# Gating the output projection's r tiles earlier, beside the last head's output loop

## The chip, the cores and the metric

The kernel runs on one core of one Trainium2 chip. A core has five engines that run side by side, each through its own list of instructions in order: TensorE (PE, matrix multiplication; PEld are its weight loads), VectorE (DVE), ScalarE (ACT), GpSimd (POOL) and SyncE (SP), which here issues nearly all transfers. The metric is device time in microseconds (us), the median of several executions. The profile comes from one more execution with the hardware profiler on.

## The reference

One layer of a sequence model, for 1024 tokens of width 1024, in float32. What the change touches:

```python
h = rmsnorm(x)
q, k, v, r, lr_f, lr_b, u, g_a, g_b = split(h @ w_in)
o = gla(q, k, v, lr_f) + gla reversed (q, k, v, lr_b)   # 4 heads, 256 channels each
o = o * rsqrt(mean(o * o) + eps) * gla_norm             # per head
o = o * silu(r)                                         # the gate
y_a = o @ w_branch_gla
```

Afterwards `y_a` is merged with a pooling branch `y_b` under sigmoid gates, projected and added to `x`, and a SwiGLU block with its own norm follows. The gate `o * silu(r)` is elementwise, so it can be computed in pieces of any order, as soon as a piece of `r` and the same piece of `o` exist.

## The kernel before, in words

**Numbers in two parts.** Every float32 operand of a large matrix product is split in two parts, high (`hh`, `wh`, `trh`) and low (`hl`, `wl`, `trl`). A product is three matmuls: high by high, low by high, high by low (`products`, L271). The high part is a cast on ScalarE, the low part a subtraction on VectorE or GpSimd (`split_to`, L200). `hT` holds the normed input, features on partitions, in 16 tiles: four groups of features, two token halves, high and low.

**The r tiles.** The 1024 columns of `r` are eight tiles of 128. Tiles 0 to 5 are "plain": for each of two token halves of 512, `feature_major` (L297) adds 8 x 3 matmuls into one PSUM bank. Tiles 6 and 7 are computed together as the first "gate unit" (`gunits[0]`), by a Strassen-like scheme: seven products instead of eight, in the order 1, 2, 6, 5, 3, 7, 4, each of 12 matmuls. Products 1, 6, 7 and 4 add onto one bank, 5 and 3 onto another; where a partial sum is wanted, ScalarE first copies it to a `ga` tile (L1497). Products 4 to 7 need differences of blocks of `hT`; these were stored to memory (`f_out`) and come back through `feature_parts` as `hs` tiles, which are split into `trh` and `trl` (L708, L699).

**Beside the plain tiles** runs the attention of the last head (`attention(3)`): decays, a backward pass of states, the scores of each token half (`scores`: a predicated copy L939 on VectorE, then the cast and subtraction that give `p`), and the output loop over eight blocks of 128 tokens (L1013). There each block is an `op` product from `p` and states, with VectorE making a new state `st` and ScalarE scaling it to `sf` and `so`. Its results are scaled, turned, stored to `o_out` and later loaded as `ol` tiles, two per head (`load_o`, L1052).

**The gate** (`gated`, L1205): ScalarE computes Silu of r, VectorE multiplies by the head's `ol` and writes an `o` tile (L1215). Head n gates tiles 2n and 2n+1; once a head's four pieces (two tiles, two token halves) are there, its two `o` tiles are queued for storing to `ob_out`. The first tiles of r come before the head outputs are at hand, so they are copied raw to an `r` tile (L1259) and wait in `raw_r`; each later plain half gates one waiting half (`put_by`, L1223) and then its own, straight from PSUM.

**What sets the order.** The order is written out by hand. All instructions are issued in the order of the Python program, and each engine keeps that order. `pump` (L162) is called after each group of three matmuls. It advances generators, which interleave the attention (`side`), the feature parts (`aside`) and weight splits (`pending`) with the matmuls; `soon` puts steps off by some pumps, `later` and `flush` queue stores on SP. The feature parts begin where the last attention has ended, in plain tile 3 or at tile 4 at the latest.

**Room.** Most tiles (`slot`, L98) share a pool of 39 equal slots: `hT` (16), the last head's q, k, decayed and turned keys, values and states, `r`, `ol`, `o`, `hs`, `trh`, `trl`, `ga`, `fraw` (raw gate weights), `wsum`. A new tile takes a slot that has come free. If that slot's last reader or transfer isn't done, the instruction that first writes the new tile waits for it, and with it everything behind on that engine.

Of the kernel before, what the change touches and what calls it, by code (L numbers as in the profile page):

```python
# [14 lines left out]
AF = mybir.ActivationFunctionType  # L15
# [5 lines left out]
KT = D // P  # L21
# [8 lines left out]
SQ = 32  # L30
# [24 lines left out]
def kernel(  # L55
# [20 lines left out]
    nc = tc.nc  # L76
# [17 lines left out]
    def name(s):  # L94
        count[0] += 1
        return f"{s}_{count[0]}"

    def slot(dtype=F32, shape=(2, HALF), s="slot"):  # L98
        return slots.tile([P, *shape], dtype, tag="slot", name=name(s))

    def t2(width=HALF, dtype=F32, s="t"):
        return tmp.tile([P, width], dtype, tag="t2", name=name(s), padded_shape=[P, HALF + 2 * PAD])
# [45 lines left out]
    side, aside = [], []  # L148
# [6 lines left out]
    def soon(delay, *steps):  # L155
        put_off.extend([delay, step] for step in steps)
# [36 lines left out]
    def finish_side():  # L193
        while side:
            for _ in side[0][0]:
                pass
            side.pop(0)
# [53 lines left out]
    def prepare():  # L251
        if not loaded:
            fetch()
        if loaded:
            ready.append(Weights(loaded.pop(0)))

            credit[0] = -2.0

    def take(ahead=True):

        if not ready:
            prepare()
        w = ready.pop(0)
        w.finish()
        if ahead:
            prepare()
        return w
# [29 lines left out]
    def feature_major(w, act, half, kts=KT):  # L297
        ps = bank(next(mm_banks))
        for k in range(kts):
            mm3(ps[:, :], w(k), act(k, half), k == 0, k == kts - 1)  # L300
        return ps
# [257 lines left out]
    def later(dst, src):  # L559
        deferred.append((dst, src))  # L560

    def flush(eng=nc.sync):
        while deferred:
            eng.dma_start(*deferred.pop(0))
# [101 lines left out]
    def feature_parts():  # L666
        todo = [(p, c) for p in (6, 5, 7, 4) for c in range(2)]
        wholes = []

        def load_sum():  # L670
            if len(wholes) < len(todo):
                p, c = todo[len(wholes)]
                wholes.append(slot(s="hs"))
                nc.sync.dma_start(wholes[-1][:, :, :], f_out[p][:, c])

        yield load_sum, None, None
        for n, (p, c) in enumerate(todo):
            yield load_sum, wholes[n][:, :, :], p
# [47 lines left out]
    def prepare_beside(jobs, every, put=PUT, lag=1, quick=0):  # L726
        aside.append([beside(chain(*jobs), every, put, lag, quick), 1 if quick else every])

    def finish_beside():
        while aside:  # L730
            for _ in aside[0][0]:
                pass
            aside.pop(0)
# [318 lines left out]
    def load_o(h):  # L1052

        o_heads[h] = [slot(s="ol") for _ in range(2)]
        for half in range(2):
            nc.sync.dma_start(o_heads[h][half][:, :, :], o_out[h][half].rearrange("(j p) t -> p j t", p=P))
# [89 lines left out]
    def bank_of(z, p):  # L1146

        if p == 1:
            z.u = bank(ps_mm)
        elif p == 5:  # L1150
            z.x = bank(ps_g)
        return bank(ps_g) if p == 2 else z.u if p in UP else z.x
# [30 lines left out]
    def product(unit, p, ps, right):  # L1183
        for k in range(4):
            mm3(
                ps[:, :], unit(p, k), tuple(t[:, k % 2, :] for t in right[p][k // 2]),
                k == 0 and p in FIRST, k == 3, p not in FIRST,
            )
# [13 lines left out]

    raw_r, oT = [], {}

    def gated(j, half, src):  # L1205

        sr = t2(s="sr")
        nc.scalar.activation(sr[:, :], src, AF.Silu)
        if j // 2 not in oT:
            oT[j // 2] = [slot(s="o") for _ in range(2)], []  # L1210
        tiles, there = oT[j // 2]

        turned = o_heads[j // 2][half][:, j % 2, :].rearrange("p (i n b) -> p n i b", i=4, b=SQ)
        dst, silu = (t.rearrange("p (n i b) -> p n i b", n=4, b=SQ) for t in (tiles[half][:, j % 2, :], sr[:, :]))
        nc.vector.tensor_tensor(dst, turned, silu, op=ALU.mult)  # L1215
        there.append((j, half))
        if len(there) == 4:
            c = j // 2 % 2
            for half, t in enumerate(tiles):
                later(ob_out[j // 4, half][:, 2 * c : 2 * c + 2, :], t[:, :, :])  # L1220
            soon(2, flush)

    def put_by():  # L1223

        if raw_r:
            gated(*raw_r.pop(0))

    BY = 3
    sums_begun = False
    for j in range(KT - 2):  # L1230
        if 2 <= j <= 4:
            load_o(j - 2)
        w = take()
        if j == 4:
            for _ in range(2):
                gunits[0].load()
        if j == 5:
            gates_ahead.step()
        if j < BY:
            whole_r = slot(s="r")  # L1240
        for half in range(2):
            if j >= BY and not sums_begun and (j > BY or not side):
                finish_side()
                finish_beside()
                prepare_beside([feature_parts()], 5, quick=2)
                sums_begun = True
            ps = feature_major(w, hT, half)
            if half == 0:
                flush()
                if j == 4:  # L1250
                    deferred.extend(last_o)
                    flush()
                elif j == 5:
                    load_o(HEADS - 1)
            elif j == KT - 3:
                for _ in range(2):
                    gunits[1].load()
            if j < BY:
                nc.scalar.copy(whole_r[:, half, :], ps[:, :])  # L1259
                raw_r.append((j, half, whole_r[:, half, :]))  # L1260
            else:
                put_by()
                gated(j, half, ps[:, :])
            if j == KT - 3 and half == 0:
                gates_ahead.step()
    for p, i, half in ((1, 0, 0), (2, 1, 0), (3, 1, 1)):
        right[p] = [hT.pair(2 * i + c, half) for c in range(2)]
# [201 lines left out]
    late = []  # L1469

    def finish_late():
        while late:
            late.pop(0)()

    class Gates:
# [12 lines left out]
        def run(self, p):  # L1488
            while len(right.get(p, ())) < 2:
                next(aside[0][0])  # L1490
            ps = bank_of(self, p)
            product(self.unit, p, ps, right)
            ps = ps[:, :]
            finish_late()
            part = {1: (0, 0), 6: (0, 1), 5: (1, 1)}.get(p)
            if part:
                nc.scalar.copy(self.row(part[0])[:, part[1], :], ps)  # L1497
                return
            i, half = {2: (0, 0), 3: (0, 1), 4: (1, 0), 7: (1, 1)}[p]
            done = self.row(i)[:, half, :]  # L1500
            if p != 4:
                add(done, ps, done)
                ps = done
            if self.kind == "r":
                if p == 4:
                    nc.scalar.copy(done, ps)
                late.append(partial(gated, KT - 2 + i, half, done))
                return
            if self.kind != "u":
                nc.scalar.activation(done, ps, AF.Sigmoid)  # L1510
            elif p == 4:
                nc.scalar.copy(done, ps)
            self.done.append((i, half))
            if self.kind == "b" and p in (7, 4):
                for at in self.done:
                    self.pooling(*at)
                self.done = []
# [450 lines left out]
    done = {}  # L1968
# [118 lines left out]
    for at, p in enumerate(OUT_ORDER):  # L2087
# [9 lines left out]
        for i in range(CLOSE if closing else n_of):  # L2097
            n = at * n_of + i
# [57 lines left out]
```

## Time and profile before

| | us |
|---|---|
| median of 3 runs (lowest, highest) | 1383.68 (1383.6, 1384.03) |
| the profiled execution's own time | 1384.49 |
| its span, first to last instruction | 1382.7 |
| TensorE busy | 1358.9 (98%) |
| VectorE / ScalarE / GpSimd busy | 857.4 / 647.3 / 754.5 |
| plain r tile 0 begins; tile 5 ends (TensorE) | 263.7; 348.6 |
| mean granted TensorE clock | 0.995 |

Lines of the profile are read so: the start in us, the duration, the engine, the line of the code, the operation, output<-inputs, shapes and number; in brackets the idle time of the engine before it and what ended it. A line of code can be a helper's, as L202 is for all subtractions. In groups, "us, times, longest" follow the pair that waits and is waited for.

### The profile page before, as it was taken

The page shows a single profiled execution, that of the slowest core. Times are in us where ns is not written, and L with a number is a line of the kernel's source. Part 1 is how long each engine was busy: PE and PEld are TensorE (multiplying, and loading weights), DVE is VectorE, ACT ScalarE, POOL GpSimd, SP SyncE. Part 2 cuts the span into 40 slices and gives each one's busy share as a digit, 9 for nine tenths or more (in the row PEclk, how much of TensorE's full clock was granted, in tenths as well). Part 3 has the DMA queues.
Part 4 walks back from the last instruction along what each step waited for, and adds up shares of the span by engine and source line. Part 5 has one row for each costly group of instructions (what it writes and reads, how often), then busy time and mean ns, then how long its engine had stood idle before and what let it go on. Part 6 is the DMA issues. An engine that isn't in the chain of part 4 may idle for free. (4 is left out here: it accounts for less than half of the span.)

```text
span 1382.7 us, 17799 instructions
## 1 busy us (share of the span) xinstructions
PE 1358.9 (98%) x6246; PEld 1128.5 (82%) x6246; DVE 857.4 (62%) x1054; ACT 647.3 (47%) x1177; POOL 754.5 (55%) x561
## 2 busy tenths in 40 slices
PE   9999999999699999999999999999999999999998
PEld 7888888888488888888888888888888888888886
DVE  6966566655645786687884856555655556343375
ACT  7365666754434445554346633333333334444353
POOL 3323723222488556668665276666666667455454
PEclk9999999999899999999999999999999999999999
DMA  6321623315777668996516355555444447985552
GB/s 225 116 86 54 186 76 104 91 51 183 228 229 253 202 212 282 365 384 219 200 62 233 121 180 175 175 175 175 154 140 142 142 146 259 387 304 188 171 213 77
DMA packets 177563, 254.60 MB, mean 184 GB/s; under 512 B 11672, under 2 KB 103360, under 8 KB 177472
## 3 DMA queue, kind: packets, MB, share of 16 engines
q1 hardware_dynamic: 177328, 253.20, 54.7%
q8 instruction: 49, 0.80, 0.2%
q14 instruction: 42, 0.34, 0.1%
q10 hardware_dynamic: 144, 0.26, 0.0%
HBM read 170.32 MB, written 83.10 MB: 183 GB/s over the span
## 5 line engine op out<-in xcount | busy, mean ns | idle before, releaser
L202 POOL TENSOR_TENSOR wl<-fs,wh 128x512 fp32r<-128x512 f32 x124 | 171.9, 1391 | 165.2 <-ACT wh L201 109.0
L274 PE MATMUL ps<-gh,wh 128*128 128x512 f32 x616 | 240.5, 390 | 0.0
L274 PE MATMUL ps<-gl,wh 128*128 128x512 f32 x616 | 239.8, 389 | 0.3 <-DVE gl L1714 0.3
L274 PE MATMUL ps<-gh,wl 128*128 128x512 f32 x616 | 239.7, 389 | 0.0
L202 POOL TENSOR_TENSOR wl<-fraw,wh 128x512 fp32r<-128x512 f32 x93 | 134.1, 1442 | 80.9 <-ACT wh L201 75.5
L202 POOL TENSOR_TENSOR ol<-gor,oh 128x1024 fp32r<-128x1024 f32 (+1 forms) x42 | 101.6, 2424 | 85.7 <-ACT oh L201 60.0
L274 PE MATMUL ps<-hh,wh 128*128 128x512 f32 x356 | 144.5, 406 | 1.4 <-ACT ga L1497 0.7
L274 PE MATMUL ps<-hh,wl 128*128 128x512 f32 x356 | 139.1, 391 | 1.2 <-POOL wl L202 1.2
L274 PE MATMUL ps<-hl,wh 128*128 128x512 f32 x356 | 138.8, 390 | 0.0
L274 PEld LDWEIGHTS ps<-gl,wh 128*128 128x128 f32 x616 | 115.7, 188 | 24.3 <-DVE gl L1714 0.7
L274 PEld LDWEIGHTS ps<-gh,wl 128*128 128x128 f32 x616 | 115.6, 188 | 24.2
L274 PEld LDWEIGHTS ps<-gh,wh 128*128 128x128 f32 x616 | 115.7, 188 | 24.0 <-DVE sums L1880 0.2
L274 PE MATMUL ps<-oh,oh 128*128 128x512 f32 x308 | 119.8, 389 | 0.0
L274 PE MATMUL ps<-ol,oh 128*128 128x512 f32 x308 | 119.8, 389 | 0.0
L274 PE MATMUL ps<-oh,ol 128*128 128x512 f32 x308 | 119.8, 389 | 0.0
L202 POOL TENSOR_TENSOR wl<-wraw,wh 128x512 fp32r<-128x512 f32 x56 | 92.3, 1677 | 44.8 <-ACT wh L201 44.7
L202 DVE TENSOR_TENSOR ol<-wor,oh 128x1024 fp32r<-128x1024 f32 (+1 forms) x42 | 62.6, 1501 | 67.6 <-ACT oh L201 55.1
L202 POOL TENSOR_TENSOR wl<-raw,wh 128x512 fp32r<-128x512 f32 x34 | 48.1, 1425 | 86.3 <-ACT wh L201 63.4
L201 ACT CAST wh<-fs 128x512 fp32r<-128x512 f32 x124 | 76.0, 614 | 26.4 <-DVE fs L1116 25.4
L274 PEld LDWEIGHTS ps<-hh,wl 128*128 128x128 f32 x356 | 66.8, 188 | 16.2 <-POOL wl L202 2.0
L274 PE MATMUL ps<-trh,wh 128*128 128x512 f32 x176 | 69.6, 396 | 9.9 <-ACT ga L1497 9.9
L274 PEld LDWEIGHTS ps<-hh,wh 128*128 128x128 f32 x356 | 67.0, 188 | 14.4 <-ACT ga L1497 1.2
(278 smaller groups left out, 3085.0 us busy)
## 6 DMA issues: line engine op xcount, KB each, us to landing
fraw<-in_w_ffn_in_dram SPq DMA_DIRECT2D x44, 512.0 KB, 7.2
gor<-g_out SPq DMA_DIRECT2D x35, 512.0 KB, 5.5
fraw<-in_w_in_dram SPq DMA_DIRECT2D x22, 512.0 KB, 5.9
g_out<-s SPq DMA_DIRECT2D x44, 256.0 KB, 2.4
wor<-t_out SPq DMA_DIRECT2D x20, 512.0 KB, 4.0
raw<-in_w_in_dram SPq DMA_DIRECT2D x36, 256.0 KB, 4.4
g_out<-g SPq DMA_DIRECT2D x33, 256.0 KB, 2.5
x<-in_x_dram SPq DMA_DIRECT2D x16, 512.0 KB, 5.4
```

Source lines behind the costliest of these rows:

```text
L201: nc.scalar.copy(hi, src)
L202: eng.tensor_tensor(lo, src, as_f32(hi), op=ALU.subtract)
L274: nc.tensor.matmul(ps, a[i], b[j], start=first and n == 0, stop=last and n == 2, skip_group_check=onto)
```

## The change

The raw wait now ends after two tiles instead of three (`BY`), so plain tile 2 is gated itself and with it tile 0; tile 3 takes tile 1 along; tiles 4 and 5 have no raw tile left to take. The point from which the feature parts may begin stays at tile 3 (`PARTS_FROM`). The loads of the head outputs 0 and 1 move from tiles 2 and 3 to tiles 1 and 2; those of heads 2 and 3 stay at tiles 4 and 5. Of a raw tile, Silu is computed in place, and so it is for the two tiles of the gate unit. In plain tile 5 the second token half comes first.

```diff
-    def gated(j, half, src):
-
-        sr = t2(s="sr")
-        nc.scalar.activation(sr[:, :], src, AF.Silu)
+    def gated(j, half, src, sr=None):
+
+        sr = t2(s="sr")[:, :] if sr is None else sr
+        nc.scalar.activation(sr, src, AF.Silu)
...
-    BY = 3
+    BY, PARTS_FROM = 2, 3
     sums_begun = False
     for j in range(KT - 2):
-        if 2 <= j <= 4:
-            load_o(j - 2)
+        for h in {1: (0,), 2: (1,), 4: (2,)}.get(j, ()):
+            load_o(h)
         w = take()
+        if j < BY:
+            whole_r = slot(s="r")
...
-        if j < BY:
-            whole_r = slot(s="r")
-        for half in range(2):
-            if j >= BY and not sums_begun and (j > BY or not side):
+        for n, half in enumerate(reversed(range(2)) if j == KT - 3 else range(2)):
+            if j >= PARTS_FROM and not sums_begun and (j > PARTS_FROM or not side):
...
             ps = feature_major(w, hT, half)
-            if half == 0:
+            if n == 0:
                 flush()
...
             if j < BY:
                 nc.scalar.copy(whole_r[:, half, :], ps[:, :])
-                raw_r.append((j, half, whole_r[:, half, :]))
+                raw_r.append((j, half, *[whole_r[:, half, :]] * 2))
             else:
                 put_by()
                 gated(j, half, ps[:, :])
-            if j == KT - 3 and half == 0:
+            if j == KT - 3 and n == 0:
                 gates_ahead.step()
...
-                late.append(partial(gated, KT - 2 + i, half, done))
+                late.append(partial(gated, KT - 2 + i, half, done, done))
```

More of the change, by code (lines that the diff above doesn't have):

```diff
@@ L1213, in gated @@
         turned = o_heads[j // 2][half][:, j % 2, :].rearrange("p (i n b) -> p n i b", i=4, b=SQ)
-        dst, silu = (t.rearrange("p (n i b) -> p n i b", n=4, b=SQ) for t in (tiles[half][:, j % 2, :], sr[:, :]))
+        dst, silu = (t.rearrange("p (n i b) -> p n i b", n=4, b=SQ) for t in (tiles[half][:, j % 2, :], sr))
         nc.vector.tensor_tensor(dst, turned, silu, op=ALU.mult)
```

## The prediction

> **What bounds the kernel now.** I read the page first, then the waits of TensorE, then the stretch around its one large wait in windows, and there ScalarE, VectorE and the SP queue in order of time.
>
> ```profile
> span 1382.7 us, 17799 instructions
> PE 1358.9 (98%) x6246; PEld 1128.5 (82%) x6246; DVE 857.4 (62%) x1054; ACT 647.3 (47%) x1177; POOL 754.5 (55%) x561
> PE   9999999999699999999999999999999999999998
> PEclk9999999999899999999999999999999999999999
> ...
> PE ps L274 <- ACT ga L1497: 10.7, 2, 9.9
> PE ps L274 <- POOL wl L202: 2.3, 4, 0.9
> ```
>
> TensorE sets the time: it is busy for 98% of the span. So a change pays only where TensorE waits, and costs only where it makes TensorE wait. Nearly all waiting stands in the eleventh slice, where the r tiles end and the gate products begin: two waits for the copy of a gate sum (`ga`, L1497), one of them 9.9 us.
>
> The windows have, after the stretch in us, the busy time (and the number) of PE, PEld, DVE, ACT and POOL, then PEclk, DMA share and GB/s:
>
> ```profile
> 295.00:303.00 8.00, 8.00 (x51) 7.06 (x49) 3.49 (x7) 2.72 (x7) 1.23 (x1) 1.00 0.00 1
> 337.70:348.60 10.90, 10.90 (x49) 8.70 (x47) 3.38 (x4) 2.90 (x4) 0.00 (x0) 1.00 0.61 183
> 348.60:356.80 8.20, 6.34 (x25) 4.27 (x24) 7.59 (x8) 3.20 (x6) 3.19 (x2) 1.00 0.88 272
> 356.80:366.70 9.90, 0.00 (x0) 0.00 (x0) 7.01 (x7) 5.38 (x9) 4.34 (x3) 0.75 0.78 228
> 366.70:374.90 8.20, 8.19 (x24) 6.28 (x24) 4.99 (x5) 2.74 (x5) 4.96 (x4) 0.67 1.01 350
> ...
> 349.28 0.50 PE L274 MATMUL ps<-hh,wh 128*128 128x512 f32 x1 [0.67 <-ACT wh L201]
> 366.71 0.80 PE L274 MATMUL ps<-trh,wh 128*128 128x512 f32 x1 [9.94 <-ACT ga L1497]
> 375.66 0.50 PE L274 MATMUL ps<-hh,wh 128*128 128x512 f32 x1 [0.73 <-ACT ga L1497]
> ```
>
> The last r tile is 48 matmuls (two token halves of 24) in 10.9 us. The next 48, products 1, 2, 6 and 5 of the first gate unit, lie between 348.6 and 374.9 and take 26.3 us. **15.4 us are lost there**: 9.94 in the wait, some 1.8 in smaller waits before it, 2.8 at the fallen clock after it (8.20 us for 24 matmuls instead of 5.45), the rest in slower starts after each wait. The 0.73 behind that is another matter: product 3 adds onto product 5's bank right after it and must wait for its copy.
>
> Why is the copy at 366.07 so late, when product 1 was done by 353.4? ScalarE and VectorE work in program order:
>
> ```profile
> 345.70 2.01 ACT L708 CAST trh<-hs 128x1024 fp32r<-128x1024 f32 x2 [9.57 <-PE ps L274]
> 348.14 0.58 ACT L1208 ACTIVATE sr<-ps 128x512 f32<-128x512 f32 x1
> 348.62 0.61 ACT L201 CAST wh<-fraw 128x512 fp32r<-128x512 f32 x1
> 357.38 1.04 ACT L708 CAST trh<-hs 128x1024 fp32r<-128x1024 f32 x1 [5.11 <-DMA ob_out<-o]
> 366.07 0.59 ACT L1497 COPY ga<-ps 128x512 f32<-128x512 f32 x1 [1.13 <-DVE fs L1116]
> ...
> 344.40 0.69 DVE L1215 TENSOR_TENSOR o<-ol,sr 128x512 f32<-128x512 f32 x1 [8.03 <-PE ps L274]
> ...
> ob_out<-o SPq DMA_DIRECT2D x8, 512.0 KB, 9.0
> ```
>
> These are waits for room, not for data. A cast to `trh` and a multiplication into an `o` tile wait for matmuls that don't feed them: those matmuls are the last readers of the `h` tiles whose slots they take over. A later cast waits 5.11 us for the store of gated tiles `ob_out`, which had 9.0 us to land. All of it comes from the pool of 39 slots being full. ScalarE stood still for 9.57 and 5.11 us, so the casts of the gate weights (348.62) came when TensorE already wanted them, and product 1's copy stood behind all of it.
>
> **The change part by part.** *Slots.* Before, r tiles 0 to 2 wait raw and are gated one per plain tile from tile 3 on, so pair (2,3) is finished only with tile 5. At the end of tile 3 the old order holds 3 raw tiles, 4 head outputs `ol` and 4 `o` tiles. The new one has gated tiles 0 to 3 by then: 4 `o` tiles are on their way out and nothing else is held, 7 slots fewer, 11 once they have landed. The eight pairs `trh`/`trl`, cast from tile 3 to tile 5, then find slots. Their four stores can go when tile 3's second multiplication ends, 332.9 by the slow pair at 329.37 below, plus the price found below: about 335 instead of 348, so the 9.0 us of landing end near 344, ahead of the critical stretch. Until then they hold up the `hs` loads and the last head's stores behind them on SP, which a full pool held up about as long before. The other edit, second half first in tile 5, frees four `h` slots one half, 24 x 0.227 = 5.45 us, sooner: those of the 8.03 and 9.57 us waits. If ScalarE is no longer blocked for long, the gate's weights are cast during tile 5 and product 1's copy follows its last matmul, 2.7 us (12 matmuls of product 2) before product 6 wants it; the casts then just ahead of it are three of 0.6 us. So I take the **whole 15.4 us** as gone; the lower bound is nothing. The 0.73 stays, its order being unchanged.
>
> *The price in the loop.* Tile 2 is now gated beside the last head's output loop. Two raw copies of 0.57 become four Silus of about 0.6 and four multiplications of 0.69, and the table load moves from 322.7 to the first of them. That is in front of the score chain, which feeds the loop's first `op` product:
>
> ```profile
> 297.89 0.51 ACT L922 ACTIVATE sb<-st,fac 128x256 f32<-128x256 f32 x1 [0.55 <-DVE st L918]
> 298.31 0.57 ACT L1259 COPY r<-ps 128x512 f32<-128x512 f32 x1
> 299.40 0.69 DVE L202 TENSOR_TENSOR p<-sc,p 128x512 fp32r<-128x512 f32 x1 [0.94 <-ACT p L201]
> 301.69 0.28 PE L274 MATMUL op<-vh,p 128*128 128x256 f32 x1
> ...
> 307.97 0.70 DVE L939 COPY_PREDICATED sc<-keep,sc 128x512 f32<-128x512 uint8 x1 [1.81 <-PE sc L934]
> 308.70 0.59 ACT L201 CAST p<-sc 128x512 fp32r<-128x512 f32 x1 [1.01 <-DVE sc L939]
> 309.32 0.69 DVE L202 TENSOR_TENSOR p<-sc,p 128x512 fp32r<-128x512 f32 x1 [0.65 <-ACT p L201]
> 309.92 0.47 DVE L918 SCALAR_TENSOR_TENSOR st<-kv,fac,so 128x256 f32<-128x256 f32 x1
> 310.43 0.51 ACT L922 ACTIVATE sf<-st,fac 128x256 f32<-128x256 f32 x1 [1.15 <-DVE st L918]
> 311.86 0.59 PE L1026 MATMUL op<-sf,qe 128*128 128x256 f32 x2
> ...
> 322.70 1.28 ACT L1208 ACT_TABLE_LOAD   x1
> 324.53 0.58 ACT L1208 ACTIVATE sr<-ps 128x512 f32<-128x512 f32 x1
> 327.07 1.25 DVE L1215 TENSOR_TENSOR o<-ol,sr 128x512 f32<-128x512 f32 x2
> 329.37 3.48 DVE L1215 TENSOR_TENSOR o<-ol,sr 128x512 f32<-128x512 f32 x2
> ```
>
> The r copy stands ahead of the score chain in program order, so both multiplications now stand ahead of COPY_PREDICATED on VectorE. The load can start at 298.40; the second Silu ends 2.41 later, as from 322.70 to 325.11, at 300.8. Its multiplication lets the copy in at about 301.5. The cast follows 0.73 later and the subtraction 0.62 after that, as from 307.97; it ends at 303.55. The `op` matmul that reads it was at 301.69 and had 1.6 us to spare; it now comes at about 303.65. TensorE, and everything queued behind that matmul, waits **2.0 us**. The bounds: 0.7 without the load; 4.2 if the two multiplications take the 3.48 of the slow pair instead of 1.25, though POOL, which was busy beside that pair, is nearly idle here.
>
> At tile 2's second half the same additions, without a load, make the next `st` about 1.0 later against the shifted loop. Its `sf`, ready at 310.94, has 0.92 us until TensorE reads it at 311.86: 0.1 us of wait. With 0.1 for the slower matmuls after a wait the price is **2.2 us**. Tile 3 costs what it cost, less a load that no engine was waiting behind.
>
> The Trainium skill ("ScalarE: Activation LUTs", What ACT_TABLE_LOAD costs) adds a drain of about 1.38 us to the 1.28 us of a load. The trace disagrees: the Silu began 1.30 us after the load's start. By the page the wait would be an estimated 3.4 us, and the time 1.4 higher.
>
> *What is hidden.* One load serves Silu together with the loop's Square and copies: there is none between the Silu's at 769.3 and the Squares at the end.
>
> ```profile
> L166 ACT ACT_TABLE_LOAD  x1: 1283/1283/1283, 769.3 to 769.3; - x1
> L2051 ACT ACTIVATE sq<-x x3: 632/632/632, 1366.5 to 1373.7; 128x512 f32<-128x512 f32 x3
> ...
> 274.06 14.55 SPq L1056 DMA_DIRECT2D ol<-o_out  x2
> ```
>
> The two loads of `ol` move up one r tile each on the SP queue, past the next tile's weights, which they delay by the 1 us of their issue. SP issued tile 3's at 274.06, when TensorE was still ahead of tile 2's 301.69, so that is covered. Before, the second pair held SP for 14.55 us until a slot came free; taken earlier, it should find one. By my count the new order fills the pool exactly (39 of 39) as the loop's first step ends. The four `o` tiles take slots that the loop has already given up, so I cost this at nothing; without that cover VectorE would stop in front of the score chain. Silu in place saves a temporary and no time; in the gate unit too.
>
> The sum: 1384.49 - 15.4 + 2.2 = 1371.3 for the profiled execution (its span is 1.8 less). That one is 0.8 above the median of 1383.68, so against the median I expect **1370.5**.
>
> **The rivals.** *Only the store's wait goes (B).* The casts, differences and copies that ScalarE did from 357.38 to 366.07 may be a chain of their own, with only the 5.11 us saved. Then 4.8 us of the gap stay, the clock still falls (2.8), and 15.4 shrinks to 15.4 - 7.6 = 7.8: 1383.68 - 7.8 + 2.2 = 1378.1. For it: ScalarE's last wait ahead of the copy is for VectorE (1.13). Against: that chain is backlog, since ScalarE had idled 9.57 us just before.
>
> *The loop's wait trips the clock (D).* At its upper bound, 4.2 + 0.2 us, TensorE might restart at half speed as it did after 366.7 and lose those 2.8 us too: 1383.68 - 15.4 + 7.2 = 1375.5. Waits under 1 us left the clock at 1.00. The Trainium skill ("TensorE: Matmul & The Clock Gate", What's actually happening) puts the half rate behind an idle window of about 3.4 us, between my value and my upper bound.
>
> *It doesn't do what it says (C).* If the slots were not the cause and product 1's copy stays where it is, only the price is left: 1383.68 + 2.2 = 1385.9, within what a measurement can tell from no change (0.2%, 2.8 us).
>
> *Slower: the 16 DMA engines become the bound (E).* Place: 335 to 352. Four stores of 0.5 MB now go out together, ahead of the last head's 1 MB, and the `hs` and `fraw` loads queue behind them. The price: 2 MB at the 350 GB/s of the busiest window are 6.0 us by which loads come later; on top of an unremoved gap and the 2.2 that is 1391.9. For it: shares of 0.88, 0.78 and 1.01 around the gap. Against: 0.61 from 337.7 to 348.6. It decides only if the share reaches 1.0 from 335 on and TensorE then waits for casts of loaded tiles, the gap having been a matter of transfers.
>
> **How the numbers follow.** Chances: forecast 0.60, B 0.18, D 0.05, C 0.08, E 0.09. The range: 1367.8 is the forecast with the loop's price at its lower bound (1.5 less) and a further 1.2 for the 0.73 wait and its slow matmuls; upward it takes in D and B, and 2.8 us for a clock that falls once more: 1380.9. C and E lie outside. Faster by over 0.2%: forecast, B and D, 0.83; within 0.2%: C, 0.08; slower: E, 0.09.
>
> **What would show it.** Right: TensorE's largest wait is no longer for `ga` at product 6; the clock stays at 1.00 through tile 5 and the gates; no `trh` cast waits for `ob_out`; a new wait of about 2 us stands at the first `op<-vh,p`, for `p`; the Silu load is at about 298. Wrong: a wait of over 4 us at product 6 (B, C), clock below 1.00 near 304 (D), a DMA share of 1.0 with ScalarE waiting for `hs` or `fraw` (E), or a VectorE multiplication in the loop that waits for a slot or for `ol`.

## The result, and the profile after

| | us | ratio to before (95% interval) |
|---|---|---|
| before, median (lowest, highest) | 1383.8 (1383.6, 1384.03) | |
| changed kernel, median of 4 | 1375.73 (1374.82, 1378.58) | 0.9945 (0.9928 to 0.9962) |
| forecast, with its range | 1370.5 (1367.8 to 1380.9) | |

The change made the kernel 8.1 us faster; 13.2 were forecast. The profiled execution took 1378.58 us, the longest of the four.

The page of the changed kernel, engines and slices:

```profile
span 1376.9 us, 17794 instructions
PE 1358.1 (99%) x6246; PEld 1128.4 (82%) x6246; DVE 858.9 (62%) x1054; ACT 646.7 (47%) x1175; POOL 755.7 (55%) x561
PE   9999999999999999999999999999999999999998
```

The 6 in TensorE's row, where the r tiles meet the gate products, is gone. What TensorE waited for, in total, times and longest, of the changed kernel:

```profile
PE ps L274 <- ACT ga L1497: 4.8, 2, 4.1
PE op L274 <- ACT p L201: 1.6, 2, 1.3
```

The wait for `ga` is less than half of the 10.7 it was, and there is a new one for `p`. Windows of this kernel (tiles 3 and 4, tile 5, products 1 and 2, products 6 and 5), and the matmuls after the two waits for `ga`:

```profile
324.00:337.00 13.00, 13.00 (x59) 10.76 (x58) 11.21 (x17) 8.07 (x13) 4.57 (x3) 1.00 0.93 293
337.00:349.00 12.00, 12.00 (x55) 9.94 (x54) 5.25 (x5) 2.05 (x3) 1.29 (x1) 1.00 0.98 278
351.00:356.80 5.80, 5.53 (x25) 4.25 (x23) 5.76 (x5) 3.82 (x6) 3.48 (x3) 1.00 1.10 351
360.60:368.90 8.30, 8.25 (x24) 6.42 (x24) 5.21 (x5) 2.78 (x6) 5.96 (x4) 0.64 0.50 178
...
360.65 0.79 PE L274 MATMUL ps<-trh,wh 128*128 128x512 f32 x1 [4.13 <-ACT ga L1497]
369.81 0.50 PE L274 MATMUL ps<-hh,wh 128*128 128x512 f32 x1 [0.68 <-ACT ga L1497]
```

Tile 5 runs into products 1 and 2 without a stop, so the smaller waits ahead of the gap are gone. At product 6 TensorE still waits 4.13 us, and then works at a mean clock of 0.64: 24 matmuls in 8.25 us instead of 5.45, or 2.8 lost.

How much each part is worth is read from where the same matmul starts in both profiles. Up to the loop they run level: the last matmul of r ahead of the first `op` product starts at 301.23 before and at 301.31 now. The last matmul of tile 5 starts 2.48 us later than before (348.22, now 350.70), product 3's first 5.85 us earlier (375.66, now 369.81). So the loop costs 2.4 us, and in the gap 2.48 + 5.85 = 8.3 of the 15.4 us are won. 7.1 are left: 4.13 of waiting, 2.8 of clock, and slower starts. 1384.49 + 2.4 - 8.3 = 1378.6, against 1378.58 measured. The account closes; what has to be explained is the 7.1.

The price in the loop, in the rows of the changed kernel:

```profile
298.51 1.28 ACT L1208 ACT_TABLE_LOAD   x1
299.80 0.63 ACT L1208 ACTIVATE r<-r 128x512 f32<-128x512 f32 x1
...
301.08 0.68 DVE L1215 TENSOR_TENSOR o<-ol,sr 128x512 f32<-128x512 f32 x1
301.68 0.69 DVE L939 COPY_PREDICATED sc<-keep,sc 128x512 f32<-128x512 uint8 x1
...
303.04 0.39 PE L274 MATMUL op<-vh,p 128*128 128x256 f32 x1 [1.35 <-ACT p L201]
303.76 0.38 PE L274 MATMUL op<-vh,p 128*128 128x256 f32 x1 [0.22 <-DVE p L202]
...
313.61 0.51 ACT L922 ACTIVATE sf<-st,fac 128x256 f32<-128x256 f32 x1 [1.15 <-DVE st L918]
314.18 0.70 PE L1026 MATMUL op<-sf,qe 128*128 128x256 f32 x2
```

The chain is the predicted one: load, two Silus, two multiplications, and only then the predicated copy, at 301.68 (forecast 301.5). TensorE waits 1.35 + 0.22 = 1.57 us, and with slower starts behind the waits its work is 2.1 us later here (the third `op<-vh,p` was at 301.69). At the second half the state `sf` is ready at 314.12 and its matmul starts at 314.18, 2.32 us later than before (311.86): another 0.2 us.

The gap's own chain, ScalarE and VectorE of the changed kernel:

```profile
342.74 1.05 ACT L708 CAST trh<-hs 128x1024 fp32r<-128x1024 f32 x1 [6.39 <-PE ps L274]
349.12 1.05 ACT L708 CAST trh<-hs 128x1024 fp32r<-128x1024 f32 x1 [4.33 <-DMA hs<-f_out]
...
359.50 0.62 ACT L201 CAST wh<-fs 128x512 fp32r<-128x512 f32 x1 [4.44 <-DVE fs L1116]
360.02 0.58 ACT L1497 COPY ga<-ps 128x512 f32<-128x512 f32 x1
...
353.74 3.45 DVE L699 TENSOR_TENSOR trl<-hs,trh 128x1024 fp32r<-128x1024 f32 x2
357.12 1.75 DVE L1215 TENSOR_TENSOR o<-ol,sr 128x512 f32<-128x512 f32 x1
358.79 0.68 DVE L1116 TENSOR_TENSOR fs<-fraw,fs 128x512 f32<-128x512 f32 x1
```

No cast waits for `ob_out` any more; the second long wait is for a load, `hs`. And the copy that TensorE wants stands behind a weight cast, which waits 4.44 us for a sum that VectorE comes to only after two differences and a multiplication.

### The profile page after: what moved, and what is told of

The parts are those of the page before. It is cut to its first block, busy times and chain, and to the rows that moved or that the text cites. A ratio compares the mean times of both kernels' runs of the same rounds, so it can differ in the third digit from the quotient of the medians.

```text
span 1376.9 us, 17794 instructions
## 1 busy us (share of the span) xinstructions
PE 1358.1 (99%) x6246; PEld 1128.4 (82%) x6246; DVE 858.9 (62%) x1054; ACT 646.7 (47%) x1175; POOL 755.7 (55%) x561
## 5 line engine op out<-in xcount | busy, mean ns | idle before, releaser
L274 PEld LDWEIGHTS ps<-hl,wh 128*128 128x128 f32 x356 | 67.0, 188 | 12.3
```

The lines of the kernel that those rows point to most:

```text
L274: nc.tensor.matmul(ps, a[i], b[j], start=first and n == 0, stop=last and n == 2, skip_group_check=onto)
```

## The experiments

Two theories at first. *Room*, the prediction's: free slots and the gap goes; what is left is some slot still taken late. The rival, *late loads*, takes up E's mechanism: with room there, the `hs` loads themselves are late, because stores and loads now crowd one queue and the 16 DMA engines. All times are medians of four executions or more, and a ratio is to the kernel before, run beside it. Unless said otherwise the comparison is with the changed kernel at 1375.73, or 1376.34 in its second measurement.

**The changed kernel again** (no edit).

> The changed kernel itself, beside the others on one chip. It should come out at 1375.7 us again, within 1374.8 to 1378.6, with a wait of about 4 us for the copy of product 1 ahead of product 6 and one of about 1.6 us for p in the loop. If the spread between executions comes from the clock, the slower ones show a lower granted clock (0.996 or 0.997 against 1.000).

1376.34 us (1375.7 to 1378.75), ratio 0.995 (0.9933 to 0.9967). SP's queue (the rows SPq are issues of transfers), then ScalarE, of this execution:

```profile
329.82 5.47 SPq L564 DMA_DIRECT2D ob_out<-o  x4
335.34 0.88 SPq L674 DMA_DIRECT2D hs<-f_out  x1
336.28 5.58 SPq L564 DMA_DIRECT2D o_out<-ot  x8
341.94 2.36 SPq L674 DMA_DIRECT2D hs<-f_out  x3
...
341.61 1.05 ACT L708 CAST trh<-hs 128x1024 fp32r<-128x1024 f32 x1 [5.64 <-DMA hs<-f_out]
348.06 1.05 ACT L708 CAST trh<-hs 128x1024 fp32r<-128x1024 f32 x1 [4.39 <-DMA hs<-f_out]
```

Both long waits of ScalarE now name the load. (The 6.39 us in the profile before this one named TensorE; but there the first load, issued at 336.44, took 5.6 to 6.3 us to land, which is when that wait ended.) The four `ob_out` stores hold SP for 5.5 us, since they wait for tile 3's multiplications; one `hs` load follows, then the last head's eight stores, and three more loads only from 341.94. ScalarE, idle since 335.97 (341.61 - 5.64), can only wait for them.

**The halves of tile 5 in their old order**, in the changed kernel.

```diff
-        for n, half in enumerate(reversed(range(2)) if j == KT - 3 else range(2)):
+        for n, half in enumerate(range(2)):
```

> The changed kernel with tile 5's token halves in their old order; nothing is left out. Theory 1 (room): ScalarE's wait of 6.39 us for the last reader of an h tile grows by the 5.45 us of a half, and the gap ahead of product 6 by as much: about 1381. Theory 2 (the hs loads, late on the SP queue): that wait would end at 348.2, before the load of hs lands at 349.1, so only the next hs load, whose slot is an h tile's too, comes later, by some 3 us: about 1378. If the order of the halves doesn't matter: 1375.7.

1376.5 us (1375.71 to 1378.08), 0.9949 (0.9934 to 0.9963): no difference. The casts wait for the loads as before (6.49 and 4.49 us), product 6 waits 4.4.

**The reversed halves alone**, in the kernel before.

```diff
-        for half in range(2):
+        for n, half in enumerate(reversed(range(2)) if j == KT - 3 else range(2)):
...
-            if half == 0:
+            if n == 0:
...
-            if j == KT - 3 and half == 0:
+            if j == KT - 3 and n == 0:
```

> The kernel before with only tile 5's token halves swapped. Theory 1 (room in the pool, by whichever tiles): the waits of 8.03 and 9.57 us for h tiles end 5.45 us sooner, the store to ob_out goes out at 343 instead of 348.4, and the gap shrinks from 9.94 to about 4.5; with the small waits before it gone that is about 7 us, 1376.5. Theory 2 (the earlier gating is what frees the room): only the waits for h tiles shorten, the wait for ob_out takes their place, and the gain is 2 us or less, 1382.

1382.36 us (1381.68 to 1383.79, 10 executions), 0.9989 (0.998 to 0.9999). ScalarE of this kernel:

```profile
344.80 1.05 ACT L708 CAST trh<-hs 128x1024 fp32r<-128x1024 f32 x1 [3.51 <-DMA o_out<-ot]
...
356.44 1.04 ACT L708 CAST trh<-hs 128x1024 fp32r<-128x1024 f32 x1 [4.03 <-DMA ob_out<-o]
```

The wait for the `h` slots becomes a wait for the next slots, those that stores free; product 6 still waits 9.3. Alone the reversal is worth 1.4 us, and beside the earlier gating nothing that can be measured. Room did matter before, but the room that counted was that of the gated tiles.

**Silu into temporaries again**, in the changed kernel.

```diff
-                raw_r.append((j, half, *[whole_r[:, half, :]] * 2))
+                raw_r.append((j, half, whole_r[:, half, :]))
...
-                late.append(partial(gated, KT - 2 + i, half, done, done))
+                late.append(partial(gated, KT - 2 + i, half, done))
```

> The changed kernel with Silu written to a temporary again, for the raw tiles and the gate unit's. As predicted it costs and saves nothing: 1376 within the spread of 1374.8 to 1378.8. If the temporaries (a pool of five) bind, a wait for one shows in the loop and the time is above 1378.

1376.28 us (1374.16 to 1378.28), 0.9945 (0.9929 to 0.9961). In place or not makes no difference, as predicted.

**Tile 2's first half gated two groups of matmuls later**, so that the score chain goes first on both engines.

```diff
-                put_by()
-                gated(j, half, ps[:, :])
+                if j == BY and n == 0:
+                    soon(2, put_by, partial(gated, j, half, ps[:, :]))
+                else:
+                    put_by()
+                    gated(j, half, ps[:, :])
```

> The changed kernel, but tile 2's first half is gated two groups of matmuls later, behind the score chain on ScalarE and VectorE; nothing is left out. If the price in the loop is the order in front of the score chain, as predicted, the waits of 1.35 and 0.22 us for p go and the time falls by 1.6: about 1374.1. If the table load or the multiplications cost wherever they stand, another wait of over 1 us comes up in the loop and the time stays at 1375.7.

1374.27 us (1373.66 to 1375.42), 0.9932 (0.9917 to 0.9947): 1.5 to 2.1 faster than the changed kernel, which fits the 1.57 of waiting and the 2.1 by which the first `op` product came later. TensorE's waits in this kernel have no line for `p` from ScalarE among the first any more, and that for `ga` stands, with 4.2 us in two waits, the longest 3.5. So the greater part of the price in the loop is settled: it comes from the order of the two chains, and two groups of matmuls take it away. The 0.2 us of the second half, whose order is the same, stay.

**The last head's eight stores on another queue**: GpSimd's, or, in a second kernel with `flush(nc.scalar)`, ScalarE's.

```diff
                 if j == 4:
                     deferred.extend(last_o)
-                    flush()
+                    flush(nc.gpsimd)
```

> The changed kernel with the last head's eight stores (o_out from ot) issued by POOL instead of SP. In the changed kernel SP spends 5.6 to 5.8 us on issuing them, and the next hs loads stand behind. Theory 2a (SP's order): those hs loads go out some 5.7 us sooner, ScalarE's wait of 4.4 us for hs goes, and with it the wait of 3.4 to 4.1 us ahead of product 6 and the fallen clock after it: about 1370.5. Theory 2b (the 16 DMA engines are full there, share 0.93 to 1.10): the loads land no sooner and the time stays near 1376.

> The same with ScalarE's queue as the issuer. Theory 2a: the same gain, 1370.5, if ScalarE's own time for eight issues (some 5.6 us as on SP) falls into its wait for the first hs load (5.6 us in the changed kernel); if the issues delay its casts instead, 1373 to 1376. Theory 2b: near 1376.

GpSimd's queue: 1377.25 us (1376.19 to 1384.32), 0.9952 (0.9934 to 0.997), if anything slower. ScalarE's: 1372.73 us (1371.78 to 1375.38), 0.9923 (0.9907 to 0.9938), 3.0 to 3.6 us faster, between the two figures of theory 2a. In both, the four `hs` loads are issued in a row. GpSimd's queue first, then ScalarE's:

```profile
337.82 9.01 SPq L674 DMA_DIRECT2D hs<-f_out  x4
334.62 4.82 POOL L564 DMA_DIRECT2D o_out<-ot  x8
351.26 1.05 ACT L708 CAST trh<-hs 128x1024 fp32r<-128x1024 f32 x1 [14.42 <-DMA hs<-f_out]
...
q0 software_dynamic: 384, 1.05, 16.6%
hs<-f_out SPq DMA_DIRECT2D x4, 512.0 KB, 12.6
```

```profile
335.04 6.75 SPq L674 DMA_DIRECT2D hs<-f_out  x4
330.56 1.49 ACTq L564 DMA_DIRECT2D o_out<-ot  x2
332.08 8.38 ACTq L564 DMA_DIRECT2D o_out<-ot  x6
...
343.25 1.05 ACT L708 CAST trh<-hs 128x1024 fp32r<-128x1024 f32 x1 [1.21 <-DMA hs<-f_out]
...
324.00:337.00 13.00, 13.00 (x59) 10.77 (x58) 10.08 (x13) 6.43 (x11) 4.56 (x3) 1.00 1.08 342
...
q10 hardware_dynamic: 2176, 1.05, 10.9%
356.54 0.50 PE L274 MATMUL ps<-trh,wh 128*128 128x512 f32 x1 [0.93 <-ACT ga L1497]
```

(The rows q0 and q10 are the queues from 325 to 360 us: packets, MB, share of the 16 engines; the `hs` row ends with the median time to landing.) The profile with GpSimd's queue is of an execution of 1384.32 us, where the other four took 1376.19 to 1378.17, so its waits are longer than usual. On GpSimd's queue all eight stores leave between 334.62 and 339.4, in the time of the loads, and the loads take 12.6 us to land instead of 6.0. The same 1.05 MB take 16.6% of the engines there (12.1% in the run below, where the loads took 10.0 us) and 10.9% on ScalarE's queue. On ScalarE's queue the stores leave from 330.56 on, while SP still stands at `ob_out`, so 324 to 337 moves 342 GB/s instead of 293; the loads land soon after, and product 6 waits 0.93. ScalarE spends 9.9 us on issuing; a Silu and a cast that the changed kernel had at 334.80 and 335.30 come at 340.51 and 341.00 for it, and no wait of TensorE grows by that. Late loads are therefore a cause of the gap, and issuing them sooner is not enough: with GpSimd's queue the second and third of the four went out 4.6 and 2.6 us sooner than in the changed kernel's profile and landed later. The Trainium skill ("DMA: Bandwidth & Descriptors", Issuing engines are not separate DMA queues) says that transfers from all three run on the same 16 engines and interleave; the run on GpSimd's queue agrees, 12.6 us against 6.0. The Trainium skill ("Trainium Kernel Development and Optimization", Key Constraints) adds that several issuers save only the issue time; here the eight stores also no longer stood behind the 5.5 us that SP spends at a wait.

**Both, with GpSimd's queue.**

> Both steps together: tile 2's first half gated behind the score chain, and the last head's stores issued by POOL. If the two waits are independent the gains add: 2.0 below the kernel with the stores moved alone, 1368.5 by theory 2a, 1374.3 by theory 2b. If the product 6 wait grows by what the loop gains, it equals the kernel with the stores moved alone.

1376.26 us (1374.87 to 1376.77), 0.9946 (0.9929 to 0.9964): the loop's gain is lost again in loads, for which one cast waits 8.61 us; product 6 waits 3.5.

**The eight stores ahead of the `ob_out` stores, on SP's queue**: is it enough that they don't stand behind a wait?

```diff
+            if j == 3 and n == 1:
+                deferred.extend(last_o)
...
-                if j == 4:
-                    deferred.extend(last_o)
-                    flush()
-                elif j == 5:
+                if j == 5:
```

> The last head's eight stores stay on SP's queue but are put ahead of the four ob_out stores; nothing else moves on any engine's order. Theory 'the queue stands still' (with the stores on ScalarE's queue the gap closed because they went out at 330.6 to 340.5 us, while SP stood at ob_out stores that wait for multiplications; a second queue as such is not needed): the stores go out at 330 to 336, the four ob_out stores right behind them, the sum loads from about 339 on in one row; the casts of loaded tiles wait less than 4 us in all, product 6 waits 0.7 to 1.5 for the copy of ga instead of 3.4 to 4.8, time 1372 to 1373.5. Rival 'a second queue': what helped was that the loads stood behind nothing on a queue of their own; here they stand behind twelve stores, the first lands later than now, product 6 waits 4 or more, time 1375.5 to 1378.

1377.56 us (1376.4 to 1379.43), 0.9958 (0.9943 to 0.9973): no gain. The waits of SP and ScalarE:

```profile
331.83 5.84 SPq L564 DMA_DIRECT2D o_out<-ot  x8
337.76 3.42 SPq L564 DMA_DIRECT2D ob_out<-o  x4
341.24 4.05 SPq L674 DMA_DIRECT2D hs<-f_out  x4
...
348.23 1.05 ACT L708 CAST trh<-hs 128x1024 fp32r<-128x1024 f32 x1 [9.40 <-PE ps L274]
```

The wait that names TensorE ends 7 us after the first load's issue, when that load lands (6.9 us here at the least). Nothing stands still on SP now, but all four loads come behind twelve stores, and two waits of 6.4 and 4.3 have become one of 9.4. "The queue stands still" falls as the whole cause: on one queue, some of these transfers were late in both orders. The rival's time came, though product 6 waited 3.57 us and not 4.

**The later gating with each of the two.**

> Tile 2's first half gated two groups of products later, and the last head's eight stores on ScalarE's queue. If the loop's price (1.57 us, gone in the first of these alone) and the gap at product 6 (4.1 to 4.8, 0.9 left in the second alone) are separate, their gains add: 1372.7 - 1.6 to 2.1 = 1370.6 to 1371.1, with no wait for p and at most 1 us for the copy of ga. If the later gating pushes the multiplications and so the ob_out stores back, as the pair with GpSimd's queue did not show (1376.3 against 1377.3), the time stays at 1372 to 1373.

> The later gating with the eight stores ahead of the ob_out stores on SP's queue. 'The queue stands still' and separate gains: ga's copy waits at most 1.5, none for p, 1370.5 to 1372. 'A second queue': 1374 to 1376, as with the later gating alone (1374.3) or a little above.

With ScalarE's queue: 1371.28 us (1370.1 to 1373.27), 0.9908 (0.9892 to 0.9925), the fastest of all, 4.5 to 5.1 below the changed kernel. Of the expected sum, 1.45 of 1.6 to 2.1 came, and product 6 still waited 2.0 in the profiled execution. With the stores first on SP: 1372.81 us (1371.98 to 1375.36), 0.9925 (0.9911 to 0.994), between the two expectations; product 6 waits 2.9. Why the stores first help beside the later gating and not without it stays open: the runs moved both the stores and the multiplications that `ob_out` waits for.

**The copy of `ga` ahead of the weight cast**, in the changed kernel; loads and stores stay.

```diff
-            if not gates_ahead.step() and at in (5, 7):
-                line_make()
-            zs[of].run(p)
+            if n == 0 and at == 0:
+                zs[of].run(p)
+                gates_ahead.step()
+            else:
+                if not gates_ahead.step() and at in (5, 7):
+                    line_make()
+                zs[of].run(p)
```

> The changed kernel with one exchange: on ScalarE the first copy of ga (the one that product 6 waits for) stands ahead of the cast of a weight sum, wh from fs, that it stands behind now; on VectorE the next weight sum stands behind one more difference of a loaded tile. Loads, stores and the loop stay. Theory 'the copy waits in ScalarE's row, not for its own data': product 1's bank has been full since 351, ScalarE comes to the copy at about 355 rather than 360, so product 6 waits 0 to 0.5 instead of 3.4 to 4.1, the clock stays, and the time is 1375.7 to 1376.3 less 4 to 5.5: 1370.5 to 1372. Rival 'the loads are late whatever the order': the casts and differences that wait for the late loads and for VectorE hold TensorE one product later, at the weights of wh and wl from fs, by 2.5 to 4 us, and the time is 1374 to 1376.5.

1373.35 us (1372.95 to 1373.98), 0.9929 (0.9913 to 0.9946). ScalarE, VectorE and TensorE of this kernel:

```profile
341.21 1.05 ACT L708 CAST trh<-hs 128x1024 fp32r<-128x1024 f32 x1 [5.49 <-DMA hs<-f_out]
347.75 1.05 ACT L708 CAST trh<-hs 128x1024 fp32r<-128x1024 f32 x1 [4.48 <-DMA hs<-f_out]
355.91 0.59 ACT L1497 COPY ga<-ps 128x512 f32<-128x512 f32 x1 [2.23 <-PE ps L274]
...
352.37 3.45 DVE L699 TENSOR_TENSOR trl<-hs,trh 128x1024 fp32r<-128x1024 f32 x2
...
356.55 0.50 PE L274 MATMUL ps<-trh,wh 128*128 128x512 f32 x1 [0.64 <-ACT ga L1497]
364.16 0.50 PE L274 MATMUL ps<-hh,wh 128*128 128x512 f32 x1 [1.86 <-ACT ga L1497]
```

The loads are as late as ever, yet product 6 waits 0.64 instead of 3.4 to 4.1, and the clock stays at 1.00. So the gap as such was the copy's place in ScalarE's row, behind a cast that waited for VectorE. What is left of it: the profile names TensorE as the copy's releaser, but product 1 had ended at about 353.2, and on VectorE two differences ended at 355.82, 0.09 before the copy. That these held it, through the room that `ga` takes, is argued, not shown. Part of the gain is given back one copy later: product 3 waits 1.86 instead of 0.68. Both waits for `ga` together fall from 4.8 to 2.5, and the time lies between the two expectations, 2.4 to 3.0 below the changed kernel (2.2 to 2.9 by the ratios, as the kernel before took 1383.13 beside it and not 1383.8).

## Why the prediction was right or wrong

*The slots and the store: right.* The `ob_out` stores went out from 330.2 to 336.4 (forecast 335) and no cast waited for them; the waits before the gap are gone.

*"I take the whole 15.4 us as gone": this step failed, 7.1 stayed.* Two sentences carried it. First, that the `hs` loads would be held up by the early stores only "about as long" as by the full pool before: with room at hand ScalarE ran on to the next limit, the loads, and waited 5.6 and 4.4 us for them, at a DMA share of 0.93 to 1.10 where it had been 0.61 and 0.88. Second, that product 1's copy would have only "three casts of 0.6" ahead of it: one of them waited 4.44 us for a sum on VectorE, which was working off the differences of the late loads. ScalarE's queue for the stores (0.93 left) and the copy moved ahead (0.64 left) each take most of the wait at product 6 away, at different links of that chain.

*The second half first: wrong as a part of the sum.* It was given the release of the 8.03 and 9.57 us waits; undone, it changes nothing, and alone it brings 1.4.

*The price in the loop: right,* 2.4 for 2.2, at the predicted place and by the predicted chain: 2.1 for 2.0 at the first half, and at the second 0.2, where a wait of 0.1 for `sf` was forecast. The multiplications took 0.7 each, far from the slow pair.

*What is hidden: right.* Silu in place is worth nothing either way. The `ol` loads found their slots: 1.33 us where there had been 14.55.

```profile
270.85 1.33 SPq L1056 DMA_DIRECT2D ol<-o_out  x2
```

*The rivals.* B came nearest: its 1378.1 is 2.4 us from the median, the forecast 5.2. It had what remains nearly by its size (4.8 in the gap and 2.8 of clock; 4.13 and 2.8 in the profiled execution), and its evidence, ScalarE's last wait being for VectorE, was the row that I set aside as backlog. The measured time lies in the range because the range was drawn to take in B, not because the sum was right. What goes away B had otherwise: the long waits for room went, and waits for loads took their place. E's condition came true, a share of about 1.0 from 335 on and casts waiting for loads, but at a smaller price, since the gap it was to be added to did go. D did not come in the changed kernel's profile, where 1.35 us in the loop left the clock at 1.00; in the profile of the run with GpSimd's queue the same wait of 1.34 us was followed by a clock of 0.50 from 303.53 to 306.95. C fell.

## What to carry to other kernels

A wait for room hides the wait behind it: before counting a gap as gone, ask when the data would arrive with all the room in the world, and count the bytes of loads and stores that would then run together. Look at the one instruction that TensorE waits for and at what stands ahead of it on its own engine; moving that one instruction up was worth nearly as much here as mending the transfers that made its engine late. Where a queue stands at a store that waits for a computation, transfers behind it can go from another engine's queue, if that engine can spare the time: from ScalarE's it brought 3 us here, from GpSimd's nothing.

## What was not expected of the hardware

**Between 2 and 4 us, the clock after a wait can't be told from its length.** Number of the next 24 matmuls that TensorE had begun 5.45 us after the wait at product 6 (24 at full clock), by the wait, from the profiled executions of the changed kernel and of its variants:

| wait, us | 0.64 | 0.93 | 2.02 | 2.92 | 3.03 | 3.44 | 3.51 | 3.51 | 3.57 | 4.03 | 4.13 | 4.38 |
|---|---|---|---|---|---|---|---|---|---|---|---|---|
| matmuls | 24 | 24 | 17 | 24 | 24 | 17 | 18 | 17 | 17 | 13 | 13 | 13 |

A wait of 2.02 us was followed by a slower clock, one of 3.03 was not. What decided in these traces is where the wait lies on a grid of steps of 3.41 us, at whose bounds alone the granted clock changes: around product 6 it was 0.50 for 3.41, 6.83 or 10.24 us. Two steps of the run with the wait of 2.02 us:

```profile
354.22:357.63 3.41, 1.48 (x6) 1.24 (x7) 3.08 (x4) 2.44 (x5) 2.13 (x2) 1.00 0.75 299
357.64:361.04 3.40, 3.40 (x9) 2.66 (x8) 3.04 (x2) 0.90 (x3) 3.14 (x3) 0.50 0.00 0
```

Nearly all of the wait fell into the first step, in which TensorE was busy for 1.48 us, or 0.43 of it; the clock fell at its end, at 357.63, though TensorE had been back at work since 356.15. The waits of 2.92 and 3.03 us were each shared by two steps (busy for 0.58 and 0.57, 0.58 and 0.53), and the clock stayed. Between 290 and 390 us of all fourteen profiles a full clock fell to half after every step with a share of 0.43 or less and after none with 0.55 or more; of four steps between, at 0.52 to 0.54, it fell after one, in the loop. Part of the spread between executions of one kernel, almost 4 us, goes with it: those of the changed kernel ran from 1374.82 us at a mean clock of 1.000 to 1378.58 at 0.996. The Trainium skill ("TensorE: Matmul & The Clock Gate", What's actually happening) gives an idle window of about 3.4 us and calls it free-running; the window and the free-running part fit these steps of 3.41 us, but a whole idle window was not needed here, where 0.43 busy was enough.

**VectorE slows beside GpSimd.** A multiplication of 128x512 took 0.68 us or 1.75, a difference of 128x1024 took 1.21 or 2.3. The longer ones overlap GpSimd's subtractions, as in the changed kernel:

```profile
354.61 3.70 POOL L202 TENSOR_TENSOR wl<-fs,wh 128x512 fp32r<-128x512 f32 x2 [2.06 <-ACT wh L201]
```

Beside it, from 353.74 to 358.87, stand the two differences (3.45) and the multiplication (1.75) on VectorE that made the sum late. The Trainium skill ("SBUF — State Buffer", SBUF: two separate sides) describes a port pair that the two engines lock in turn; that the lock is the cause here was not tested.
